# Forgetting attention by pairs of heads: the values stationary in float32, the exponentials moving

## The chip, the cores and the metric

The kernel runs on one core of a Trainium2 chip, alone. The metric is the device time of one execution in microseconds (us); the number to forecast is the median of several executions. The engines are TensorE (PE in the rows; PEld is its weight load), VectorE (DVE), ScalarE (ACT), GpSimd (POOL) and SyncE (SP), which issues the DMAs here. Each engine works through a list of its own, in an order that is fixed when the program is built; the engines meet at semaphores.

## The reference

One layer with two branches on the same projection of x (2048 tokens, 1024 columns), a gate, an output projection, and a last RMSNorm. The change is in the second branch, attention over 8 heads of 64 columns with a forget gate:

```python
h = rmsnorm(x, norm_g[l]);  p = h @ w_in[l]          # 1024 -> 3208 + 1024 gate columns
y_rw  = rwkv7_branch(...)                             # recurrence over time, 8 heads
# fox_branch, per head and block of queries:
q = rmsnorm(heads(p[..., 0:512]), q_g);  k = rmsnorm(heads(p[..., 512:1024]), k_g)
c = jnp.cumsum(jax.nn.log_sigmoid(fl + b_f), axis=1)
s = jnp.einsum('bhqd,bhkd->bhqk', qb, kf) * scale + cb[..., :, None] - c[:, :, None, :]
s = jnp.where(mask, s, -jnp.inf)
o = jnp.einsum('bhqk,bhkd->bhqd', jax.nn.softmax(s, axis=-1), vf)
y = jnp.concatenate([y_rw, y_fox], axis=-1) * jax.nn.silu(gate)
x = x + y @ w_out[l];  return rmsnorm(x, final_g)
```

## The kernel before

The program has three parts. **Part one** projects: the RWKV columns (line 254, `pj_r`) with the work that prepares the recurrence, and between them, as filler, the attention's q, k and v (line 332, `pf`) and the gates (line 254, `pj_g`). **Part two** is the recurrence over 32 chunks of 64 tokens, `chain` (`pX`, `pY`, `pU`, `pS`, lines 737 to 763), which goes step by step from TensorE to VectorE or ScalarE and back; attention is the work that stands between its steps. **Part three** is `out_tile`: 16 tiles of 128 tokens, each with 48 matmuls of 512 columns (line 1111, `po`).

Where an instruction stands on its engine is decided by a scheduler of the framework when the program is built. The source gives the order of priority (`chain_all` ahead of `attend`), the scheduler then mixes the streams by durations it assumes.

Attention has two steps per head. `head_max` finds the largest score of each query: matmuls into `sq` (lines 947 and 950) and a maximum of each on VectorE (line 951). `head_out` then goes through 4 blocks of 512 queries; block `qb_` has `4 * qb_ + 4` tiles `j` of 128 keys. For each tile it forms the scores `st` with two float16 matmuls of 512 columns (lines 998 and 999; the high and low halves of q and k are spread over the rows) and, on the diagonal, a mask (line 1002). ScalarE takes the exponential into float32 `p32` (line 1006), ScalarE or VectorE rounds it to float16 `ph` (lines 1008 and 1010), GpSimd or VectorE forms the rest `pl` (line 1012). TensorE then holds a 128x128 piece of `ph` or `pl` stationary, and the values move through it, 64 or 65 columns in float16:

```python
nc.tensor.matmul(pv[:, qq, 0:65], ph[:, s_], vh[:, j, 0:65], ...)   # line 1016
nc.tensor.matmul(pv[:, qq, 0:64], ph[:, s_], vl[:, j], ...)         # line 1018
nc.tensor.matmul(pv[:, qq, 0:65], pl[:, s_], vh[:, j, 0:65], ...)   # line 1020
```

Column 65 of the values is one, so the sum of the exponentials comes with them. On the diagonal the matrices are narrower: `c0` columns are left out. Heads 0 to 5 go one after the other, heads 6 and 7 block by block together, so that `out_tile` can start.

Of the kernel before, what the change touches and what calls it, by code (L numbers as in the profile page):

```python
# [9 lines left out]
F32 = mybir.dt.float32  # L10
# [25 lines left out]
VS = 2.0 ** -20  # L36
# [3 lines left out]
def hymba_body(tc, x, norm_g, w_in, rw_mu, rw_w_up, rw_w0, rw_a_up, rw_a0, rw_k_k, rw_k_a, rw_r_k,  # L40
# [7 lines left out]
    with ctx:  # L48
# [13 lines left out]
        d_q = [dram(f"d_q{i}", [512, S], F16) for i in range(2)]  # L62
        d_k = [dram(f"d_k{i}", [512, S], F16) for i in range(2)]
        d_v = [dram(f"d_v{i}", [4, 128, 2, 16, 66 - 2 * i], F16) for i in range(2)]
        d_l = dram("d_l", [NB, 128, 2, TB])
        d_yr = dram("d_yr", [512, S])
        d_gate = dram("d_gate", [1024, S])
        d_nc = [dram(f"d_nc{i}", [8, S], F16) for i in range(2)]
        d_gs = dram("d_gs", [4, S], F16)
        d_yf = dram("d_yf", [S, 512])  # L70
# [150 lines left out]
        def load_tiles(name, offs):  # L221

            iall = wp.tile([128, 6], F32, name="ia_" + name, tag="ia", bufs=2)
            ws = [(wp.tile([128, KT, 128], F16, name=f"wh_{name}{i}", tag="wh", bufs=3),
                   wp.tile([128, KT, 128], F16, name=f"wl_{name}{i}", tag="wl", bufs=3)) for i in range(len(offs))]
            prep_w(name, offs, "r", ws, iall)
            return ws, iall
# [58 lines left out]
        def fox_turn(p, b, j0, qkn, qkt):  # L286
# [12 lines left out]
            if j0:  # L299
                pc = slice(p * 128, p * 128 + 128)  # L300
                for i, d in ((0, d_q), (1, d_k)):
                    for a in range(2):
                        nc.sync.dma_start(d[a][pc, b * TB:b * TB + TB], qkt[i][:, a])

        def fox_proj(p, fw, w):
# [10 lines left out]
            for b in range(NB):  # L316
# [3 lines left out]
                vh = F("vh" + u, "vh", (128, 2, 4, 66), F16)  # L320
                vl = F("vl" + u, "vl", (128, 2, 4, 64), F16)
                nc.gpsimd.memset(vh[:, :, :, 64:66], 1.0)
                qkt = [F(f"qkt{u}_{i}", f"qt{i}", (128, 2, TB), F16) for i in range(2)]
                qkn = []
                for j in range(4):
# [20 lines left out]
                    nc.scalar.activation(vh[:, :, j, 0:64], pv, AF.Copy, scale=VS)  # L346
                    nc.vector.scalar_tensor_tensor(vl[:, :, j], pv, VS, vh[:, :, j, 0:64], ALU.mult, ALU.subtract)
# [5 lines left out]
                for i, t in ((0, vh), (1, vl)):  # L353
                    nc.sync.dma_start(d_v[i][p, :, :, 4 * b:4 * b + 4].rearrange("q a j c -> q a (j c)"),
                                      t.rearrange("q a j c -> q a (j c)"))
# [25 lines left out]
        groups = [("f", 0), ("f", 1), ("f", 2), ("g", 0), ("g", 3), ("g", 6), ("f", 3)]  # L381
# [385 lines left out]
        def group_norm(sg, yt):  # L767
# [25 lines left out]
            nc.sync.dma_start(d_yr[:, t0:t0 + 256].rearrange("(p q) t -> q p t", q=128), gt)  # L793
# [36 lines left out]
        with c2:  # L830
# [30 lines left out]
            gs = A("gs", "nct", (32, S // 16), F16)  # L861
            nc.vector.memset(gs, GS)
            nc.sync.dma_start(d_gs[2:4].rearrange("o (j q) -> (o j) q", q=128), gs)
            gs = A("gz", "nct", (32, S // 16), F16)
            nc.vector.memset(gs, 0.0)
            nc.sync.dma_start(d_gs[0:2].rearrange("o (j q) -> (o j) q", q=128), gs)
# [4 lines left out]
            def decay_setup(p):  # L871
# [37 lines left out]
                nch = [A(f"nch{p}_{i}", f"nch{i}", (32, 128), F16) for i in range(2)]  # L909
                nc.vector.tensor_copy(nch[0], nct)  # L910
                nc.vector.tensor_tensor(nch[1], nct, nch[0], ALU.subtract)
                for i in range(2):
                    nc.sync.dma_start(d_nc[i][hs].rearrange("h (j q) -> (h j) q", q=128), nch[i])

            def v_setup(h):

                vi = ap_.tile([128, 1], F32, name=f"vi{h}", tag="vi", bufs=2)
                ts(vi, iscv[:, h:h + 1], 1.0 / VS, ALU.mult)
                vh = ap_.tile([128, 16, 66], F16, name=f"va{h}", tag="va", bufs=2)
                vl = ap_.tile([128, 16, 64], F16, name=f"vb{h}", tag="vb", bufs=2)  # L920
                nc.sync.dma_start(vh, d_v[0][h // 2, :, h % 2])
                nc.sync.dma_start(vl, d_v[1][h // 2, :, h % 2])
                return vh, vl, vi

            def head_max(h):

                qb = ap_.tile([128, S], F16, name=f"qb{h}", tag="qb", bufs=3)
                km = ap_.tile([128, S], F16, name=f"km{h}", tag="km", bufs=2)
                r = slice(h * 64, h * 64 + 64)
                nc.sync.dma_start(qb[0:64], d_q[0][r])  # L930
                nc.sync.dma_start(qb[64:66], d_gs[2:4])
                nc.sync.dma_start(km[0:64], d_k[0][r])
                for i in range(2):
                    nc.sync.dma_start(km[64 + i:65 + i], d_nc[i][h:h + 1])
                mx = ap_.tile([128, 16, 4], F32, name=f"mx{h}", tag="mx", bufs=2)
                nc.vector.memset(mx, -3e38)
                for i in range(16):
                    nb = i // 4 + 1
                    cut = [round((i + 1) * 128 * b / nb / 32) * 32 for b in range(nb + 1)]
                    for b in range(nb):  # L940
# [6 lines left out]
                        nc.tensor.matmul(ps[:, :w], qb[0:66, i * 128:i * 128 + 128], km[0:66, ks],  # L947
# [10 lines left out]
                gh = ap_.tile([16, 128], F16, name=f"gh{h}", tag="gh", bufs=2)  # L958
                gl = ap_.tile([16, 128], F16, name=f"gl{h}", tag="gl", bufs=2)
                nc.vector.tensor_copy(gh, pg)  # L960
                nc.vector.tensor_tensor(gl, pg, gh, ALU.subtract)
                return qb, gh, gl

            def head_loads(h, qb, gh, gl):

                qa = ap_.tile([128, S], F16, name=f"qa{h}", tag="qa", bufs=2)
                ka = ap_.tile([128, S], F16, name=f"ka{h}", tag="ka", bufs=2)
                kb = ap_.tile([128, S], F16, name=f"kb{h}", tag="kb", bufs=2)
                r = slice(h * 64, h * 64 + 64)
                nc.sync.dma_start(qa[0:64], d_q[0][r])  # L970
                nc.sync.dma_start(qa[64:128], d_q[1][r])
                nc.sync.dma_start(ka[0:64], d_k[0][r])
                nc.sync.dma_start(ka[64:128], d_k[0][r])
                nc.sync.dma_start(kb[0:64], d_k[1][r])
                nc.sync.dma_start(kb[64:68], d_gs)
                nc.sync.dma_start(qb[66:67].rearrange("o (j q) -> o j q", q=128), gh)
                nc.sync.dma_start(qb[67:68].rearrange("o (j q) -> o j q", q=128), gl)
                return qa, ka, qb, kb, *v_setup(h)

            def head_out(h, qa, ka, qb, kb, vh, vl, vi, blocks=range(4), last2=False):  # L980
                for qb_ in blocks:
                    nj = 4 * qb_ + 4
                    q0 = qb_ * 512
                    u = f"{h}_{qb_}"
                    be = ap_.tile([128, 16], F32, name="be" + u, tag="be", bufs=2)
                    nc.vector.tensor_scalar(be[:, :nj], c_[:, h, :nj], cref[:, h, 4 * qb_:4 * qb_ + 1], -1.0,
                                            ALU.subtract, ALU.mult)
                    pv = ps_v.tile([128, 4, 66], F32, name="pv" + u, tag="v")
                    for j in range(nj):
                        o = max(j - 4 * qb_, 0)  # L990
# [10 lines left out]
                        if diag:  # L1001
                            nc.tensor.matmul(ps[:, c0:c0 + 128], identb, mkT, start=False, stop=True)
# [155 lines left out]
```

## Time and profile before

| | |
|---|---|
| median of 3 runs | 1707.08 us (1707.0 to 1711.47) |
| the execution that was profiled | 1709.08 us, span 1707.4 us |
| TensorE | busy 1575.2 us, 92% of the span |
| VectorE, ScalarE, GpSimd | 71%, 49%, 45% of the span |
| mean granted clock of TensorE | 0.96 of 2.4 GHz |

The span goes from the first to the last instruction; 1.7 us lie around it. A matmul counts as busy from its start until its result is out, and matmuls overlap, so two that start 0.03 us apart may each be shown as 0.19 us long. How much TensorE can still take is therefore read from the distance between starts, not from its busy share.

### The profile page before, as it was taken

Reading aid. Unit: us, or ns where it says so; the run is one execution under the profiler, and the core shown is the slowest. Engines: PE = TensorE matmul, PEld = TensorE weight load, DVE = VectorE, ACT = ScalarE, POOL = GpSimd, SP = SyncE. Lnnn points to the kernel's source line nnn. Section 1 sums busy time; section 2 is a strip of 40 time slices with the busy share of each in tenths; the row PEclk is TensorE's granted clock in tenths of the full one; section 3 lists DMA queues with packets and bytes.
Section 4 is the critical chain, followed back from the end, with each engine's and each line's share of the span. In section 5 each row is a group of like instructions: output and inputs, shape, how many; then the busy total and the mean of one; then the engine's idle time right before and its main releaser. Section 6 shows DMA issues by size and latency. Waiting matters only on the chain. (4 is left out here: it accounts for less than half of the span.)

```text
span 1707.4 us, 36607 instructions
## 1 busy us (share of the span) xinstructions
PE 1575.2 (92%) x14182; PEld 974.5 (57%) x14182; DVE 1210.0 (71%) x2614; ACT 839.9 (49%) x1583; POOL 766.9 (45%) x838
## 2 busy tenths in 40 slices
PE   4899799899998999999999999899999998899998
PEld 2455355455544564445453566566666665567886
DVE  4866568975888669743844678588999997975443
ACT  5644444445433454445343247566776677564221
POOL 5754554545345543532201135455666666663000
PEclk9899899999998999999999999899999998899999
DMA  6432232233213242322234029666879633733452
GB/s 180 124 100 87 97 114 87 87 112 122 103 69 118 82 143 74 117 96 106 96 102 130 26 63 253 158 150 159 186 169 208 144 99 79 214 99 103 164 173 75
DMA packets 211983, 207.74 MB, mean 122 GB/s; under 512 B 53664, under 2 KB 173472, under 8 KB 211296
## 3 DMA queue, kind: packets, MB, share of 16 engines
q1 hardware_dynamic: 211808, 205.39, 42.1%
q8 instruction: 112, 1.84, 0.5%
q14 instruction: 63, 0.52, 0.1%
HBM read 123.34 MB, written 81.94 MB: 120 GB/s over the span
## 5 line engine op out<-in xcount | busy, mean ns | idle before, releaser
L1012 POOL TENSOR_TENSOR pl<-p,ph 128x512 f16<-128x512 f32 (+3 forms) x216 | 234.5, 1095 | 175.1 <-ACT ph L1010 70.3
L1006 ACT ACTIVATE p<-st,be 128x512 f32<-128x512 f32 (+1 forms) x320 | 193.5, 621 | 125.5 <-PE st L999 32.1
L951 DVE TENSOR_REDUCE mx<-sq 128x1 f32<-128x384 f32 (+6 forms) x320 | 184.5, 600 | 22.3 <-PE sq L947 11.6
L332 PE MATMUL pf<-fh_f,hhi 128*128 128x386 f16 x512 | 171.3, 335 | 2.1 <-DVE fl L348 1.0
L332 PE MATMUL pf<-fl_f,hhi 128*128 128x386 f16 x512 | 170.2, 332 | 1.9 <-POOL fl_f L219 1.9
L332 PE MATMUL pf<-fh_f,hlo 128*128 128x386 f16 x512 | 170.3, 333 | 0.0
L254 PE MATMUL pj_r<-hhi,wh_r 128*128 128x512 f16 x384 | 147.7, 385 | 1.3 <-ACT wh_r L218 1.2
L254 PE MATMUL pj_r<-hlo,wh_r 128*128 128x512 f16 x384 | 147.6, 384 | 0.0
L254 PE MATMUL pj_r<-hhi,wl_r 128*128 128x512 f16 x384 | 147.4, 384 | 0.0
L332 PEld LDWEIGHTS <-hhi 128*128 128x128 f16 x1024 | 100.1, 100 | 78.6 <-issue 14.6
L341 POOL TENSOR_TENSOR fr<-ft,nhalf 128x4 f32<-128x4 f32 x64 | 65.8, 1029 | 173.9 <-DVE ft L101 167.8
L1016 PE MATMUL pv<-va,ph 128*128 128x65 f16 x1088 | 133.4, 197 | 9.6 <-DVE ot L1026 7.6
L1020 PE MATMUL pv<-va,pl 128*128 128x65 f16 x1088 | 130.2, 197 | 4.6 <-POOL pl L1012 2.5
L1018 PE MATMUL pv<-vb,ph 128*128 128x64 f16 x1088 | 132.5, 195 | 0.0
L1010 ACT ACTIVATE ph<-p 128x512 f16<-128x512 f32 (+3 forms) x220 | 121.0, 561 | 13.1 <-PE pv L1020 6.8
L254 PEld LDWEIGHTS <-wh_r 128*128 128x128 f16 x768 | 74.9, 99 | 87.3 <-issue 6.5
L999 PE MATMUL st<-qb,kb 68*128 68x512 f16 (+1 forms) x320 | 114.6, 361 | 10.4 <-DMA qb<-gl 10.2
L998 PE MATMUL st<-qa,ka 128*128 128x512 f16 (+1 forms) x320 | 114.3, 360 | 6.9 <-ACT p L1006 3.9
L1016 PEld LDWEIGHTS <-ph 128*128 128x128 f16 x1088 | 102.9, 99 | 26.6 <-DVE ot L1026 9.9
L947 PE MATMUL sq<-km,qb 66*128 66x384 f16 (+6 forms) x320 | 107.0, 353 | 10.1 <-DVE mx L951 5.2
L1020 PEld LDWEIGHTS <-pl 128*128 128x128 f16 x1088 | 102.6, 99 | 22.6 <-POOL pl L1012 5.7
L1018 PEld LDWEIGHTS <-ph 128*128 128x128 f16 x1088 | 103.0, 100 | 7.7 <-issue 1.2
(378 smaller groups left out, 4068.4 us busy)
## 6 DMA issues: line engine op xcount, KB each, us to landing
d_ga<-ga SPq DMA_DIRECT2D x32, 256.0 KB
d_gl<-gl SPq DMA_DIRECT2D x32, 256.0 KB
d_nk<-nkt SPq DMA_DIRECT2D x32, 256.0 KB
d_gate<-gv SPq DMA_DIRECT2D x32, 256.0 KB
G<-d_ga SPq DMA_DIRECT2D x32, 256.0 KB
G<-d_gl SPq DMA_DIRECT2D x32, 256.0 KB
NK<-d_nk SPq DMA_DIRECT2D x16, 512.0 KB
xr<-in_x_dram SPq DMA_DIRECT2D x16, 512.0 KB
```

Source lines behind the costliest of these rows:

```text
L254: nc.tensor.matmul(ps, a[:, kt, o:o + 128], h[:, kt, :], start=n == 0, stop=n == 3 * KT - 1)
L332: nc.tensor.matmul(ps, a[:, kt, js], w[:, kt, :], start=n == 0, stop=n == 3 * KT - 1)
L947: nc.tensor.matmul(ps[:, :w], qb[0:66, i * 128:i * 128 + 128], km[0:66, ks], start=True, stop=not last)
L951: nc.vector.tensor_reduce(mx[:, i, b:b + 1], ps[:, :w], AX.X, ALU.max)
L998: nc.tensor.matmul(ps[:, c0:], ka[:, k0:k0 + 128], qa[:, q0 + c0:q0 + 512], start=True, stop=False)
L999: nc.tensor.matmul(ps[:, c0:], kb[0:68, k0:k0 + 128], qb[0:68, q0 + c0:q0 + 512], start=False, stop=not diag)
L1006: nc.scalar.activation(p32[:, c0:], ps[:, c0:], AF.Exp, bias=be[:, j:j + 1])
L1010: nc.scalar.activation(ph[:, c0:], p32[:, c0:], AF.Copy)
L1012: eng.tensor_tensor(pl[:, c0:], p32[:, c0:], ph[:, c0:], ALU.subtract)
L1016: nc.tensor.matmul(pv[:, qq, 0:65], ph[:, s_], vh[:, j, 0:65], start=j == 0 and qq == 0, stop=False, skip_group_check=True)
L1018: nc.tensor.matmul(pv[:, qq, 0:64], ph[:, s_], vl[:, j], start=False, stop=False, skip_group_check=True)
L1020: nc.tensor.matmul(pv[:, qq, 0:65], pl[:, s_], vh[:, j, 0:65], start=False, stop=fin, skip_group_check=True)
```

## The change

Attention goes by pairs of heads. `p32` is not split any more. The values of a tile of keys, 128x64 in float32, are now the stationary operand, head 0 of the pair in the left half of the array's columns and head 1 in the right half, and the float32 exponentials move through them, up to 512 columns in one matmul. The result has 64 columns of head 0 in partitions 0 to 63 and those of head 1 in 64 to 127, which is the layout that the output projection needs. The sums of the exponentials are formed by adding the tiles on VectorE and GpSimd into `acc` (the first tile's), and a float32 matmul with ones brings the sum over keys (`normalise`). Its reciprocal is `exp(-ln)` with one step of refinement; the gate is multiplied in here, so that `out_tile` loads one finished `y`.

```diff
-                        nc.scalar.activation(p32[:, c0:], ps[:, c0:], AF.Exp, bias=be[:, j:j + 1])
-                        if j % 4 < 2 if last2 else j % 4 == 2:
-                            nc.vector.tensor_copy(ph[:, c0:], p32[:, c0:])
-                        else:
-                            nc.scalar.activation(ph[:, c0:], p32[:, c0:], AF.Copy)
-                        eng = nc.vector if j % 3 == 1 else nc.gpsimd
-                        eng.tensor_tensor(pl[:, c0:], p32[:, c0:], ph[:, c0:], ALU.subtract)
-                        for qq in range(o, 4):
...
-                            nc.tensor.matmul(pv[:, qq, 0:65], ph[:, s_], vh[:, j, 0:65],
-                                             start=j == 0 and qq == 0, stop=False, skip_group_check=True)
...
+                    def values(j, c0, pt):
+                        for h, (o0, o1) in enumerate(HR):
+                            nc.tensor.matmul(pv[o0:o1, c0:], ops[h][2][:, j, :], pt[h][:, c0:],
+                                             start=j == 0, stop=j == nj - 1, skip_group_check=True)
+                        if j:
+                            for h in range(2):
+                                e = nc.vector if (h if alt else (2 * j + h) % 3 == 0) else nc.gpsimd
+                                e.tensor_tensor(acc[h][:, c0:], acc[h][:, c0:], pt[h][:, c0:], ALU.add)
...
+                            nc.scalar.activation(pt[h][:, c0:], ps[:, c0:], AF.Exp, bias=be[h][:, j:j + 1])
...
+                        pend.append((j, c0, pt))
+                        if j:
+                            values(*pend.pop(0))
+                        if j == 2 and rest:
+                            rest.pop()()
+                    values(*pend.pop(0))
+                    yv = ap_.tile([128, 512], F32, name=f"yv{u}", tag="yv", bufs=2)
+                    nc.scalar.activation(yv, pv, AF.Copy, scale=vi)
+                    nc.gpsimd.tensor_tensor(yv, yv, gt, ALU.mult)
...
+            def normalise(u, yv, acc, rows, qs):
+
+                pd = ps_s.tile([128, 512], F32, name=f"pd{u}", tag="s")
+                for h, (o0, o1) in enumerate(HR):
+                    nc.tensor.matmul(pd[o0:o1], ones[:, 0:64], acc[h], start=True, stop=True)
+                rd = ap_.tile([128, 512], F32, name=f"rd{u}", tag="rd")
+                nc.scalar.activation(rd, pd, AF.Ln)
+                nc.scalar.activation(rd, rd, AF.Exp, scale=-1.0)
+                nc.gpsimd.tensor_tensor(yv, yv, rd, ALU.mult)
+                nc.vector.tensor_tensor(rd, pd, rd, ALU.mult)
+                nc.vector.scalar_tensor_tensor(yv, rd, 2.0, yv, ALU.subtract, ALU.mult)
+                nc.sync.dma_start(d_y[rows, qs], yv)
```

Beside this, q and k are stored per head with their extra rows, so that each is loaded with fewer, larger DMAs (q per block of queries, 4 buffers each); in part one the values are stored once in float32 instead of twice in float16 (one VectorE instruction less per tile of line 332); `out_tile` loses four transposes, one multiplication and two loads per tile; the gates of the attention's columns are projected earlier; the weight tiles `wh` and `wl` come from another pool.

The order of TensorE's instructions before, in part two, in attention of head 3 (names: `st3_1_3` scores of head 3, block 1, tile 3; `pv3_0` its result of block 0; `sq4` the maxima of head 4):

```order
L998 LDWEIGHTS ka3_14779
L998 MATMUL st3_1_3_15932<-qa3_14778,ka3_14779 128x512
L999 LDWEIGHTS kb3_14780
L999 MATMUL st3_1_3_15932<-qb3_10130,kb3_14780 128x512
L947 LDWEIGHTS qb4_14623
L947 MATMUL sq4_9_1_14689<-km4_14624,qb4_14623 128x448
L1016 LDWEIGHTS ph3_0_0_15795
L1016 MATMUL pv3_0_15789<-va3_14791,ph3_0_0_15795 128x65
L1018 LDWEIGHTS ph3_0_0_15795
L1018 MATMUL pv3_0_15789<-vb3_14792,ph3_0_0_15795 128x64
L1020 LDWEIGHTS pl3_0_0_15796
L1020 MATMUL pv3_0_15789<-va3_14791,pl3_0_0_15796 128x65
```

All of it uses the whole width of the array, and three short matmuls with the values follow one another for each 128 queries.

The same place after the change, attention of pair 1 (`va2` and `va3` are the values of its two heads, `pv1_2` the result of block 2 for both, in 64 partitions each; `pd1_1` the sums of block 1; `pU18` is a step of the recurrence):

```order
L1022 MATMUL st1_2_2_1_14200<-qb1_2_1_14167,kb3_13717 128x512
L1004 MATMUL pv1_2_14171<-p321_2_1_1_14183,va3_13719 64x512
L744 MATMUL pU18_12630<-xs18_12619,zc4_12323 64x64 x8
L964 MATMUL pd1_1_14208<-p321_1_0_0_13833,ones_8320 64x512
L964 MATMUL pd1_1_14208<-p321_1_0_1_13834,ones_8320 64x512
L1004 MATMUL pv1_2_14171<-p321_2_2_0_14194,va2_13713 64x512
L1021 LDWEIGHTS ka2_13709
L1021 MATMUL st1_2_3_0_14220<-qa1_2_0_14157,ka2_13709 128x512
L1022 LDWEIGHTS kb2_13711
L1022 MATMUL st1_2_3_0_14220<-qb1_2_0_14160,kb2_13711 128x512
L1004 MATMUL pv1_2_14171<-p321_2_2_1_14195,va3_13719 64x512
L932 LDWEIGHTS qm5_8_14048
```

The matmul of tile 2 with `va2` and the one with `va3`, which the source writes one after the other, stand apart here, with scores of the whole width between them.

After the recurrence, in pair 3, some of them stand together:

```order
L1004 MATMUL pv3_2_15923<-p323_2_0_0_15924,va6_15653 64x512
L1004 MATMUL pv3_2_15923<-p323_2_0_1_15925,va7_15659 64x512
L1004 MATMUL pv3_2_15923<-p323_2_1_0_15934,va6_15653 64x512
L1004 MATMUL pv3_2_15923<-p323_2_1_1_15935,va7_15659 64x512
L1021 LDWEIGHTS ka7_15655
```

Here the left and the right half follow each other directly. Over the whole program there are 320 matmuls with values and 32 with ones; 58 pairs of a left and a right one stand together, and 236 stand alone.

## Rows read from the trace of the kernel before

**Rows 1.** The page's first part: busy us, share, instructions of each engine.

```profile
PE 1575.2 (92%) x14182; PEld 974.5 (57%) x14182; DVE 1210.0 (71%) x2614; ACT 839.9 (49%) x1583; POOL 766.9 (45%) x838
```

**Rows 2.** Stretches: busy us (count) of PE, PEld, DVE, ACT, POOL; clock; DMA share; GB/s.

```profile
0.00:1019.00 1019.00, 937.61 (x6389) 515.02 (x6390) 688.43 (x1587) 448.40 (x824) 431.03 (x512) 0.96 0.31 101
1019.00:1707.00 688.00, 637.54 (x7795) 459.47 (x7793) 521.57 (x1028) 391.55 (x760) 335.84 (x327) 0.96 0.60 152
```

**Rows 3.** Busy time by stretch: a piece of part two, one of part three.

```profile
1250.00:1300.00 50.00, 48.11 (x799) 34.24 (x800) 49.27 (x101) 32.52 (x64) 30.43 (x31) 1.00 0.78 176
1650.00:1700.00 50.00, 50.00 (x228) 41.05 (x226) 20.02 (x36) 10.61 (x25) 2.69 (x4) 1.00 0.32 111
```

**Rows 4.** Waits of TensorE from 1019 us on, the two longest.

```profile
PE st L999 <- DMA qb<-gl: 10.2, 2, 7.5
PE pv L1016 <- DVE ot L1026: 7.6, 5, 2.2
```

**Rows 5.** Groups by line from 1019 us on, TensorE: count, busy us, mean ns.

```profile
L1016 PE MATMUL pv<-va,ph 128*128 128x65 f16 x1078 | 132.0, 197 | 9.6 <-DVE ot L1026 7.6 <-DVE ph L1008 1.5 <-ACT ph L1010 0.4
...
L998 PE MATMUL st<-qa,ka 128*128 128x512 f16 (+3 forms) x312 | 111.7, 360 | 6.1 <-ACT p L1006 3.9 <-issue 1.8
L1111 PE MATMUL po<-woh,yh 128*128 128x512 f32 x256 | 102.0, 400 | 0.8 <-DVE woh L1078 0.4 <-ACT yh L1101 0.4
...
L947 PE MATMUL sq<-km,qb 66*128 66x448 f16 (+5 forms) x271 | 90.5, 355 | 5.3 <-DVE mx L951 3.6 <-DMA d_yr<-gg 0.8 <-DMA km<-d_nc 0.4
...
L737 PE MATMUL pX<-SV,G 128*64 128x64 f32 x512 | 25.0, 233 | 0.0
...
L1095 PE MATMUL pt<-ident,yf 128*128 128x128 f32 x64 | 9.9, 272 | 0.0
```

**Rows 6.** Timeline of TensorE: start us, us, what.

```profile
1198.76 0.38 PE L998 MATMUL st<-qa,ka 128*128 128x512 f16 x1
1198.98 0.38 PE L999 MATMUL st<-qb,kb 68*128 68x512 f16 x1
1199.29 0.69 PE L737 MATMUL pX<-SV,G 128*64 128x64 f32 x16
```

**Rows 7.** The same timeline, asked from the end of that group on.

```profile
1199.74 0.23 PE L737 MATMUL pX<-SV,G 128*64 128x64 f32 x2
1199.91 0.20 PE L1020 MATMUL pv<-va,pl 128*128 128x65 f16 x1
```

**Rows 8.** Timeline of TensorE, twelve starts between the two rows left out.

```profile
1201.12 0.20 PE L1016 MATMUL pv<-va,ph 128*128 128x65 f16 x1
...
1201.52 0.19 PE L1018 MATMUL pv<-vb,ph 128*128 128x64 f16 x1
```

**Rows 9.** Timeline of TensorE in part one, float32 in four quarters of the array.

```profile
353.51 0.28 PE L541 MATMUL pb<-ga,bk 64*64 64x128 f32 x2
353.53 0.28 PE L544 MATMUL pk<-ga,bk 64*64 64x128 f32 x2
353.62 0.28 PE L541 MATMUL pb<-ga,bk 64*64 64x128 f32 x2
353.64 0.28 PE L544 MATMUL pk<-ga,bk 64*64 64x128 f32 x2
```

**Rows 10.** Groups by line from 1019 us on, the other engines.

```profile
L1012 POOL TENSOR_TENSOR pl<-p,ph 128x512 f16<-128x512 f32 (+3 forms) x212 | 231.1, 1100 | 171.3 <-ACT ph L1010 69.4 <-DVE ph L1008 42.1 <-PE pv L1020 21.7
...
L1010 ACT ACTIVATE ph<-p 128x512 f16<-128x512 f32 (+2 forms) x215 | 118.3, 562 | 13.1 <-PE pv L1020 6.8 <-PE pv L1018 3.4
...
L1012 DVE TENSOR_TENSOR pl<-p,ph 128x512 f16<-128x512 f32 (+3 forms) x102 | 86.1, 844 | 8.5 <-ACT ph L1010 4.6 <-POOL pl L1012 1.9 <-PE st L999 0.7
L1008 DVE CAST ph<-p 128x512 f16<-128x512 f32 (+1 forms) x98 | 55.8, 575 | 20.1 <-ACT p L1006 12.5 <-PE pv L1020 4.0 <-PE pv L1018 3.1
...
L792 POOL TENSOR_TENSOR gg<-ysq,gg 128x512 f32<-128x512 f32 x16 | 22.7, 1420 | 14.1 <-DVE ysq L790 12.5 <-DVE gm L955 0.8 <-PE pv L1020 0.8
L787 DVE TENSOR_TENSOR ysq<-yt,ysq 128x512 f32<-128x512 f32 x16 | 13.5, 843 | 0.2 <-ACT ysq L786 0.2
```

More of the change, by code (lines that the diff above doesn't have):

```diff
@@ new lines, in hymba_body @@
+            rest = []
+            def normalise(u, yv, acc, rows, qs):
[9 more added lines that the diff above has]
+                nc.sync.dma_start(d_y[rows, qs], yv)
@@ L981, in head_out, with pair_out @@
+            def pair_out(p, ops, alt, blocks):
+                vi = ap_.tile([128, 1], F32, name=f"vi{p}", tag="vi", bufs=2)
+                for h, (o0, o1) in enumerate(HR):
+                    ts(vi[o0:o1], iscv[o0:o1, 2 * p + h:2 * p + h + 1], -1.0, ALU.mult, eng=nc.gpsimd)
                 for qb_ in blocks:
@@ new lines, in pair_out @@
+                    u = f"{p}_{qb_}"
+                    be, q1s, q2s = [], [], []
+                    for h in range(2):
+                        hd_ = 2 * p + h
+                        b = ap_.tile([128, 16], F32, name=f"be{u}_{h}", tag="be", bufs=4)
+                        nc.vector.tensor_scalar(b[:, :nj], c_[:, hd_, :nj], cref[:, hd_, 4 * qb_:4 * qb_ + 1], -1.0,
+                                                ALU.subtract, ALU.mult)
+                        be.append(b)
+                        q1 = ap_.tile([128, 512], F16, name=f"qa{u}_{h}", tag="qa", bufs=4)
+                        for o0, o1 in HR:
+                            nc.sync.dma_start(q1[o0:o1], d_qh[hd_, 0:64, qs])
+                        q2 = ap_.tile([128, 512], F16, name=f"qb{u}_{h}", tag="qb", bufs=4)
+                        nc.sync.dma_start(q2[0:66], d_ql[hd_, :, qs])
+                        q1s.append(q1)
+                        q2s.append(q2)
@@ new lines, in pair_out @@
+                        for h in range(2):
+                            kk, km = ops[h][0:2]
+                            psp, tg = (ps_q, "q") if alt and h else (ps_s, "s")
+                            ps = psp.tile([128, 512], F32, name=f"st{u}_{j}_{h}", tag=tg)
+                            nc.tensor.matmul(ps[:, c0:], kk[:, k0:k0 + 128], q1s[h][:, c0:], start=True, stop=False)
+                            nc.tensor.matmul(ps[:, c0:], km[0:66, k0:k0 + 128], q2s[h][0:66, c0:],
+                                             start=False, stop=not diag)
+                            if diag:
+                                nc.tensor.matmul(ps[:, c0:c0 + 128], identb, mkT, start=False, stop=True)
+                            nc.scalar.activation(pt[h][:, c0:], ps[:, c0:], AF.Exp, bias=be[h][:, j:j + 1])
@@ new lines, in pair_out, with top, bottom @@
+                    rest.append(partial(normalise, u, yv, acc, slice(512 + p * 128, 640 + p * 128), qs))
+            def heads():
+                def top(h):
+                    if h < 8:
+                        if h % 2 or h == 0:
+                            if (h + 1) // 2 < 4:
+                                decay_setup((h + 1) // 2)
+                        head_max(h)
+                def bottom(p, blocks):
+                    if blocks[0] == 0:
+                        for h in (2 * p, 2 * p + 1):
+                            ops[h] = head_loads(h)
+                    h = 2 * p
+                    pair_out(p, ops[h:h + 2], p == 3, blocks)
+                ops = [None] * 8
+                top(0)
+                yield
+                top(1)
+                yield
+                for p in range(4):
+                    top(2 * p + 2)
+                    bottom(p, (0, 1))
+                    top(2 * p + 3)
+                    bottom(p, (2, 3))
+                    if p == 3:
+                        rest.pop()()
```

199 lines of the change are left out of this document (66 added, 133 removed).

## The prediction

> **What bounds the kernel now.** The page's first part comes first: TensorE is busy for 1575 us, 92% of the span, the others for at most 71% [rows 1]. That figure counts matmuls until their results are out, so I split the span where the last projection ends, at 1019 us, and ask how much TensorE could still take behind it, where the change acts. There lie 688 us, of which TensorE is busy for 637.5 [rows 2].
>
> Distances between starts tell what it really does there. A float16 matmul of 512 columns takes 0.22 us, by two scores [rows 6] and by 228 matmuls in 50 us of part three, where TensorE never pauses [rows 3]; that is 0.43 ns a column. The short matmuls with the values follow each other every 0.031 us, 13 steps in 0.40 us [rows 8]; their weight loads are hidden. The recurrence runs in part of the array: the first 14 of 16 records start within 0.45 us, two by two, so a pair takes 0.064 us [rows 6, 7]. Entering such a group costs 0.09 us more than the next score would (0.31 against 0.22) [rows 6]; from its last two records to the next whole-width matmul 0.17 us pass, 0.10 more than a pair takes [rows 7]. I count 0.095 us for each change of width.
>
> With the order's counts the 688 us hold: scores and masks 124 us (294,912 columns in all, 312 of 320 tiles here [rows 5]); maxima 57 (155,648 columns, 271 of 320 [rows 5]); values 3,234 x 0.031 = 100; recurrence 1,272 x 0.064 = 82; output 768 x 0.22 = 169; the rest (sums of squares, transposes) 16; changes of width 374 x 0.095 = 36. Together 584 us. So 104 us are free on TensorE, spread out: its longest named waits are 10.2 and 7.6 us [rows 4]. In part two VectorE is at least as tight, 49.3 us of 50 busy [rows 3], so there neither engine alone sets the pace; in part three it is TensorE.
>
> **The change part by part.** *Taken from TensorE:* the 3,234 short matmuls, 100 us, and the 64 transposes of the output tiles, at most their 9.9 us in flight [rows 5]; I take 7.
>
> *Given to TensorE:* 320 float32 matmuls with values and 32 with ones, 155,648 columns. The trace has no such matmul with 512 columns. The recurrence's `pX` has the same form, 128 rows and 64 columns of the array in float32, and shows 512 records for 256 matmuls [rows 5]: two records each. In part one, four records of 128 columns in four quarters of the array start almost together, and the next four 0.11 us later [rows 9]. By that a record of 512 columns takes 0.44 us and a matmul 0.88. By the 64-column pairs it would be 8 x 0.064 x 2 = 1.02; by the step from 64 to 128 columns (0.046 us), 2 x (0.064 + 7 x 0.046) = 0.77. I take 0.86, close to rows 9, whose records are the longer ones.
>
> The two heads use the two halves of the columns and overlap if they stand next to each other, as the records of `pX` do, which start in pairs [rows 6, 7]. The order says that mostly they don't: 58 pairs stand together (25,728 columns each half), 236 matmuls alone (105,216 columns), with whole-width scores behind them, and the next whole-width matmul waits until the half is through [rows 7]. So 130,944 columns / 512 x 0.86 = 220 us, between 197 and 263 by the two bounds. Were all 352 in pairs, it would be 77,824 / 512 x 0.86 = 131 us.
>
> The Trainium skill has a rule for the gain: "TensorEngine Tiling (Array Packing)", Performance Considerations, gives column tiling with a stationary side of at most 64 columns a factor of two, which is the 131 us. It has another that speaks against it here: "TensorE: Matmul & The Clock Gate", Part 3, says that matmuls start and end in program order, so a half that stands alone finds no partner, which is the 220 us.
>
> *Changes of width:* 732 instead of 374 from the projection's end on, 358 x 0.095 = 34 us. *Order:* a few tiles of scores and maxima that stood ahead of the projection's end now stand behind it: 4 us more here and as much less before. TensorE behind the projection: 584 - 100 - 7 + 220 + 34 + 4 = 735 us. That is more than the 688 us that this stretch took with all its waits.
>
> *The other engines* get room. ScalarE loses the roundings, 118 us, and gets 48 instructions in the shape of one of them, about 30 us: 392 becomes some 304 [rows 2, 10]. VectorE loses 86 and 56 us of splitting and gets 108 of the 288 additions at 0.84 us or less and 32 steps of the normalisation: 522 becomes about 500 at most, less by the division of `ot` that I leave out [rows 2, 10]. GpSimd loses 231 us and gets 180 additions and 32 products at 1.42 us or less: 336 becomes at most 406 [rows 2, 10]. All stay far below 735, so their gains are worth nothing where TensorE is full; they only make its waits fewer. The additions into `acc` are off the path: the values' matmul reads the exponentials, not the sums, and the sum is asked for a block later. The DMAs carry about the same bytes; with 0.60 of the DMA engines' time taken in the stretch [rows 2] I cost them at nothing, covered by the longer stretch; if a pair's first q comes late, it is again a wait like the 10.2 us over two times [rows 4].
>
> *Waits that remain:* none at best, 104 us at worst. TensorE's list is now fuller and the others emptier, so I take 30. *The part before the projection's end:* 1019 less the 4 us, 1015; one VectorE instruction less per tile frees an engine busy 688 of 1019 us [rows 2] and is costed at nothing.
>
> Sum: 1015 + 735 + 30 = 1780 us of span, against 1707.4. The profiled execution is 1.7 us above its span and 2.0 above the median of the runs; both fall out, so **1780 us**, 4% slower.
>
> **The rivals.** *A, the halves overlap anyway (faster).* The array or its queue lets a half that stands alone run beside other work, for instance the left one beside the next right one past the scores between. Then values and sums cost 131 instead of 220 us, and the stretch 646 + 30: 1015 + 676 = 1691. For it: the pairs of `pX` overlap fully. Against it: after a group in part of the array the next whole-width matmul starts 0.10 us late, not early [rows 7]. It decides where 73 of the 89 us come back, four fifths of the lone columns. The skill's factor of two, named above, is this case. Chance 0.11.
>
> *B, the free time takes it all (no change).* Waits vanish and a matmul costs 0.77: 735 - 23 + 1015 = 1727; even this is slower than before, so a time within 0.3% needs half of A as well. Chance 0.04.
>
> *C, the waits stay (still slower).* TensorE now has matmuls of 0.86 us in its list, and behind each one the recurrence's next step queues. If recurrence and exponentials then wait for one another as often as now, the 104 us remain: 1015 + 735 + 104 = 1854. For it: 227 of the 352 float32 matmuls stand between the first and the last step of the recurrence, whose results VectorE and ScalarE wait for. Against it: these two have become emptier, and the tile's exponentials are asked for only one tile later. Chance 0.13.
>
> *The forecast*, 1735 to 1825: chance 0.72.
>
> **How the numbers follow.** A measurement of this kernel tells about 0.3% from no change, some 5 us. Slower: forecast and C, 0.85; same: 0.04 with B; faster: A, 0.11. The range runs from 1727 (price and waits at their lower ends) to 1855 (C): A, half of B and a little above C lie outside. The price's upper bound alone would give 1823.
>
> **What the profile would show.** The matmuls with the values as records of 0.43 us between starts, two per matmul, 0.86 us for a lone half and the same for a pair together; 0.095 us at each change of width; a TensorE that never pauses from 1015 us on, with VectorE, ScalarE and GpSimd emptier; part three beginning later. If lone halves take 0.43 us, A is right; if TensorE pauses for 100 us, C is. The forecast would also be wrong if float32 streams faster at 512 columns than at 128, which no row shows.

## The result, and the profile after

| | median of runs (lowest to highest) | profiled execution | its span |
|---|---|---|---|
| before | 1709.28 us (1707.0 to 1712.1) | 1709.08 us | 1707.4 us |
| after | 1876.72 us (1876.07 to 1878.18) | 1876.21 us | 1874.2 us |

The ratio is 1.098 (95% interval 1.0957 to 1.1003): slower, as forecast, but by 167 us and not by 71; 1877 lies above the range (1727 to 1855).

The page of the kernel after, its first and fourth part, which answers to [rows 1]:

```profile
span 1874.2 us, 30633 instructions
...
PE 1732.3 (92%) x11558; PEld 913.3 (49%) x11558; DVE 1148.1 (61%) x2350; ACT 764.7 (41%) x1395; POOL 781.8 (42%) x834
...
PE 43%; DMA 4%; DVE 1%; SPq 1%; issue 0%; ACT 0%; DVEq 0%; POOLq 0%; ACTq 0%
```

TensorE has the same share as before and everyone else less. The stretches before and behind the projection's end, now at 1022 us, answer to [rows 2] (columns as there):

```profile
0.00:1022.00 1022.00, 933.22 (x6333) 513.34 (x6334) 677.03 (x1518) 442.37 (x813) 428.04 (x495) 0.97 0.32 102
1022.00:1874.00 852.00, 799.10 (x5228) 399.93 (x5225) 471.05 (x833) 322.32 (x583) 353.81 (x339) 0.95 0.47 124
```

Nearly all of the loss lies behind the projection, 852 us in place of 688; the projection itself ends 3 us later. The same stretch in two pieces:

```profile
1022.00:1125.00 103.00, 69.71 (x590) 39.05 (x587) 46.91 (x109) 17.48 (x36) 17.90 (x23) 0.64 0.81 171
1125.00:1850.00 725.00, 712.26 (x4566) 347.02 (x4565) 417.81 (x712) 301.95 (x539) 334.81 (x315) 1.00 0.44 120
```

For the first 103 us TensorE stands still for a third of the time, at a granted clock of 0.64 on average; then it is busy for 712 of 725 us at a granted clock of 1.00, the full 2.4 GHz. Its waits from 1022 us on, which answer to [rows 4] (total, times, longest):

```profile
PE st L1022 <- DMA qb<-d_ql: 21.5, 2, 20.7
PE pX L732 <- DMA d_ql<-qkt: 5.9, 1, 5.9
PE sq L932 <- DMA qm<-d_qh: 5.3, 4, 2.8
PE pU L744 <- DMA zc<-d_z: 4.1, 1, 4.1
```

The longest is pair 0's first score, held up from 1084 to 1105 us by the query operand with head 1's maxima. The values' matmuls in the timeline (start, us in flight, what):

```profile
1155.39 0.38 PE L1022 MATMUL st<-qb,kb 66*128 66x512 f16 x1
1155.69 1.07 PE L1004 MATMUL pv<-p,va 128*64 128x512 f32 x2
1156.70 0.39 PE L1021 MATMUL st<-qa,ka 128*128 128x512 f16 x1
...
1159.40 0.33 PE L758 MATMUL pY<-AR,SV 64*64 64x64 f32 x2
1159.66 0.36 PE L932 MATMUL sq<-km,qm 68*128 68x448 f16 x1
```

A lone value matmul is two records, and from its start to the next whole-width matmul 1.01 us pass; it also starts 0.30 us behind the score where a score would start after 0.22 [rows 6].

For a balance that doesn't count overlap twice I went through TensorE's records behind the projection's end in order of start, and gave each the distance to the next start, less what lay behind its own end ("nothing in flight"). Sums in us; e1, e2 and so on are the runs of the next section. The last two columns are the mean granted clock of the stretch and an estimate of what its time at the granted clock of 0.50 cost: for each record there, its distance less the mean distance of records of the same form at 1.00 in the same run. That cost is contained in the columns of work.

| kernel | scores, maxima | values, sums | recurrence | output | rest | nothing in flight | clock | cost of half clock |
|---|---|---|---|---|---|---|---|---|
| before | 203 | 113 | 119 | 181 | 21 | 44 | 0.96 | 18 |
| after | 227 | 249 | 127 | 181 | 13 | 48 | 0.95 | 23 |
| e1 | 224 | 167 | 125 | 181 | 15 | 54 | 0.93 | 36 |
| e2 | 254 | 110 | 117 | 181 | 19 | 27 | 0.98 | 11 |
| e13 | 307 | 106 | 114 | 181 | 19 | 18 | 0.99 | 5 |
| e8 | 287 | 251 | 130 | 181 | 13 | 41 | 0.95 | 25 |
| e6 | 236 | 256 | 135 | 180 | 15 | 45 | 0.93 | 41 |
| e14 | 229 | 251 | 128 | 181 | 15 | 39 | 0.95 | 27 |
| e9 | 226 | 163 | 123 | 181 | 16 | 59 | 0.92 | 43 |
| e10 | 217 | 157 | 116 | 180 | 15 | 51 | 0.95 | 26 |
| e12 | 243 | 62 | 125 | 183 | 20 | 81 | 0.87 | 65 |
| e15 | 200 | 102 | 118 | 183 | 23 | 64 | 0.92 | 36 |

Work rose by 797 - 637 = 160 us, where the prediction's terms make 735 - 584 = 151. Nothing in flight stayed: 44 became 48. So did the cost of the half clock, 18 and 23: it stood in the kernel before as well, and the prediction's prices, all from rows at the full clock, leave it out.

### The profile page after: what moved, and what is told of

It reads as the page before. It is cut to its first block, busy times and chain, and to the rows that moved or that the text cites. A ratio compares the mean times of both kernels' runs of the same rounds, so it can differ in the third digit from the quotient of the medians.

```text
span 1874.2 us, 30633 instructions
## 1 busy us (share of the span) xinstructions
PE 1732.3 (92%) x11558; PEld 913.3 (49%) x11558; DVE 1148.1 (61%) x2350; ACT 764.7 (41%) x1395; POOL 781.8 (42%) x834
## 5 line engine op out<-in xcount | busy, mean ns | idle before, releaser
L1026 ACT ACTIVATE p<-st,be 128x512 f32<-128x512 f32 (+3 forms) x320 | 193.9, 622 | 262.3 <-PE st L1022 141.9
L1009 POOL TENSOR_TENSOR p<-p,p 128x512 f32<-128x512 f32 (+3 forms) x180 | 208.0, 1159 | 206.3 <-ACT p L1026 179.5
L1004 PE MATMUL pv<-p,va 128*64 128x512 f32 (+3 forms) x640 | 270.1, 556 | 0.2
L936 DVE TENSOR_REDUCE mx<-sq 128x1 f32<-128x512 f32 (+6 forms) x320 | 186.1, 605 | 102.1 <-PE sq L932 58.4
L1022 PE MATMUL st<-qb,kb 66*128 66x512 f16 (+3 forms) x320 | 112.1, 352 | 21.5 <-DMA qb<-d_ql 21.5
L1021 PE MATMUL st<-qa,ka 128*128 128x512 f16 (+3 forms) x320 | 113.6, 357 | 8.9 <-DMA qa<-d_qh 3.9
L932 PE MATMUL sq<-km,qm 68*128 68x512 f16 (+6 forms) x320 | 108.3, 374 | 13.1 <-DMA qm<-d_qh 5.3
L1123 PE MATMUL po<-woh,yh 128*128 128x512 f32 x256 | 101.7, 397 | 0.0
L1123 PE MATMUL po<-wol,yh 128*128 128x512 f32 x256 | 101.4, 396 | 0.0
L1123 PE MATMUL po<-woh,yl 128*128 128x512 f32 x256 | 100.4, 393 | 0.0
```

The source lines that it names most:

```text
L932: nc.tensor.matmul(ps[:, :w], qm[0:68, i % 8 * 128:i % 8 * 128 + 128], km[0:68, ks], start=True, stop=not last)
L936: nc.vector.tensor_reduce(mx[:, i, b:b + 1], ps[:, :w], AX.X, ALU.max)
L1004: nc.tensor.matmul(pv[o0:o1, c0:], ops[h][2][:, j, :], pt[h][:, c0:], start=j == 0, stop=j == nj - 1, skip_group_check=True)
L1009: e.tensor_tensor(acc[h][:, c0:], acc[h][:, c0:], pt[h][:, c0:], ALU.add)
L1021: nc.tensor.matmul(ps[:, c0:], kk[:, k0:k0 + 128], q1s[h][:, c0:], start=True, stop=False)
L1022: nc.tensor.matmul(ps[:, c0:], km[0:66, k0:k0 + 128], q2s[h][0:66, c0:], start=False, stop=not diag)
```

## The experiments

Thirteen kernels ran, each beside the kernel before. Where runs were not timed beside each other, differences of a few us are read by their ratios to the kernel before.

### e1_dep: value matmuls next to each other

```
+ with tc.high_priority():
      for h, (o0, o1) in enumerate(HR):
-         nc.tensor.matmul(pv[o0:o1, c0:], ...)
+         mm = nc.tensor.matmul(pv[o0:o1, c0:], ...)
+         if h == 0:   # ex: the second head's exponential
+             tc.add_manual_dep(mm.ins, ex, ...)
```

> The first of a tile's two value matmuls waits for the second head's exponential too, and both go ahead of other work, so that they stand next to each other in TensorE's stream: 170 adjacent pairs and 12 lone ones (the sums' matmuls counted) in place of 58 and 236, 728 changes of tile width in place of 912. Theory 1 (TensorE sets the pace from 1125 us on, a lone value matmul takes as long as an adjacent pair, some 1.0 us at 512 columns by the spacing in the trace, about 0.9 at the mean 446 columns of the lone ones, and a change of width 0.095): 112 fewer slots x 0.9 and 184 x 0.095 less, -117 us, so 1760 us (1745 to 1775). Theory 2 (the halves don't work at the same time even when adjacent): only the changes of width, some -17 us, 1860. Theory 3 (TensorE is late for other engines or transfers, which keep their pace): half or less of the 117, 1820 to 1870.

Measured: 1795.69 us, ratio 1.050 (1.0462 to 1.0538). That is 81 us less than the changed kernel: most of theory 1's 117, though above its range (1745 to 1775), too much for theory 2, and below theory 3's range. The timeline of this run:

```profile
1162.52 1.08 PE L1005 MATMUL pv<-p,va 128*64 128x512 f32 x4
1163.54 0.39 PE L1024 MATMUL st<-qa,ka 128*128 128x512 f16 x1
```

Four records, two matmuls, take 1.02 us to the next start, where the changed kernel's lone two records took 1.01. Values and sums fall from 249 to 167 us in the balance. Of the 36 us that are missing from the 117, some 13 are the half clock (36 in place of 23 in the balance) and 6 more time with nothing in flight. A wait of this run is new: the pair waits for the second exponential (groups by line: busy us, mean ns, idle before).

```profile
L1005 PE MATMUL pv<-p,va 128*64 128x512 f32 (+3 forms) x640 | 162.3, 569 | 13.1 <-ACT p L1029 12.7
```

### e2_double and e13_triple: what the kernel before can take up

```
- nc.tensor.matmul(ps[:, c0:], ka[...], qa[...], start=True, stop=False)
+ for i in range(2):        # range(3) and stop=i < 2 in e13_triple
+     nc.tensor.matmul(ps[:, c0:], ka[...], qa[...], start=True, stop=i == 0)
```

> The kernel before with the first score matmul of each tile issued twice (the first result is overwritten, the output is unchanged): 320 more whole-width matmuls, 139,264 columns, at the 0.22 us for 512 columns of the trace 60 us, and up to 10 us more for their weight loads. Theory 1 (the kernel before has next to no free time on TensorE behind the projection: 44 us with nothing in flight, and those in waits that stay): +55 to +70 us, 1765 to 1780. The prediction's own step (104 us free, of which the change takes some 70 and leaves 30 in waits): the 60 to 70 us go into free time for the most part, +0 to +25 us, 1710 to 1735.

> The kernel before with the first score matmul of each tile issued three times; issued twice it took 1736 us for 1711, so that of some 55 us of work added 25 to 30 showed. Theory 1 (the kernel before can take up some 30 us on TensorE, and that is used up by the first copy): the second copy costs 45 to 60 us more, 1780 to 1796. Theory 2 (it takes up half of what is added up to 74 us or more, as the prediction's sum has it): 25 to 30 us more, 1760 to 1768.

Measured: 1735.87 us (ratio 1.0143, 1.0116 to 1.0171) and 1780.18 us (1.041, 1.0372 to 1.0447). The first copy cost 25 us, at the upper edge of the prediction's step and far from theory 1; the second cost 44, at the lower edge of its theory 1. Each copy adds some 52 us of scores in the balance, and nothing in flight goes from 44 to 27 to 18. The stretch behind the projection in e2, where TensorE is busy for 681 of 716 us:

```profile
1024.00:1740.00 716.00, 681.28 (x8107) 483.54 (x8105) 509.00 (x1027) 396.74 (x758) 332.21 (x326) 0.98 0.57 146
```

The same in e13, 727 of 752:

```profile
1024.00:1776.00 752.00, 727.22 (x8413) 506.75 (x8411) 511.82 (x1025) 400.79 (x758) 325.74 (x326) 0.99 0.54 139
```

So the kernel before can take up some 35 us of score matmuls (104 added, 69 shown), most of it with the first copy: not none, and not 74. By the balance, 26 us come out of the time with nothing in flight; the other records become 14 us shorter, since less of the stretch runs at half clock (cost 18, then 5); and the projection's end, 4 us later, takes 4 back.

### e8_double: what the changed kernel can take up

The same edit on the changed kernel's `kk`, `q1s` matmul.

> The changed kernel with the first score matmul of each tile issued twice, the same extra work that cost the kernel before 25 us (1736 against 1711). Theory 1 (in the changed kernel TensorE works without a break from 1125 us on, so that nothing more can be taken up there): +50 to +65 us, 1927 to 1942. Theory 2 (it takes up as much as the kernel before did): +20 to +30 us, 1897 to 1907.

Measured: 1933.58 us, ratio 1.1286 (1.1253 to 1.1318): 52 us more than the changed kernel by the ratios, 57 by the medians, for 60 added in the balance. Theory 1 holds: next to nothing is taken up. Two stretches of this run:

```profile
1021.00:1125.00 104.00, 75.45 (x629) 42.25 (x628) 49.38 (x113) 17.98 (x37) 20.25 (x25) 0.64 0.84 173
1125.00:1905.00 780.00, 769.96 (x4833) 374.88 (x4830) 410.84 (x705) 305.04 (x538) 330.75 (x313) 0.99 0.41 110
```

The standstill at the start is there as before: TensorE's next instruction in its order, a score, waits 18.8 us there for the query operand, and the copies stand behind it.

### e4_noadd: without the sums

The additions `acc + p32` are left out (one addition of 1 for each row of blocks in their place), so the sums are not the reference's.

> The changed kernel with the tile-by-tile sums of exponentials left out (each head's accumulator only gets 1 added once per row of blocks), so that VectorE and GpSimd lose some 290 additions of up to 512 elements, and the exponentials' buffers come free with the value matmul; the matmuls are all there. Theory 1 (the sums run beside TensorE, which sets the pace): 0 to -10 us, 1867 to 1877. Theory 2 (the sums set the pace: they hold the exponentials' buffers and VectorE and GpSimd): -30 us or more, 1847 or less.

Measured: 1868.24 us, ratio 1.0927 (1.0897 to 1.0957); 8 us less. Theory 1: the sums hide behind TensorE.

### e3_queue: the late operand from another queue

```
- nc.sync.dma_start(d_ql[h, 64:66]..., gh)
+ (nc.scalar if h < 2 else nc.sync).dma_start(d_ql[h, 64:66]..., gh)
- nc.sync.dma_start(q2[0:66], d_ql[hd_, :, qs])
+ (nc.sync if p else nc.scalar).dma_start(q2[0:66], d_ql[hd_, :, qs])
```

> The changed kernel with the store of heads 0 and 1's maxima and the loads of pair 0's second query operands issued from ScalarE's queue instead of SyncE's. In the trace after, head 1's maxima are ready at 1081 us, their store is issued at 1094 behind recurrence loads, the operands are issued at 1102.6 and TensorE waits for them 20.7 us, to 1104.5. Theory 1 (the place in SyncE's queue makes it late): -12 to -18 us, 1859 to 1865. Theory 2 (the DMA engines, 77 to 113% busy there, make it late wherever it is issued): -5 us at most, 1872 to 1877.

Measured: 1882.16 us, ratio 1.100 (1.0975 to 1.1026), no gain, and above the ranges of both theories. The maxima are ready at 1082 us in this run; ScalarE's timeline goes on:

```profile
1093.77 0.33 ACTq L946 DMA_DIRECT2D d_ql<-gh  x1
1094.15 0.63 ACT L88 ACTIVATE ysh<-ysq 128x512 fp32r<-128x512 f32 x1 [12.12 <-DMA G<-d_ga]
1101.86 2.52 ACTq L994 DMA_DIRECT2D qb<-d_ql  x3
```

On the new queue the store is issued hardly earlier than on SyncE's in the changed kernel (1094.3), and the load at 1101.9 (1102.6). In the 78 us ahead the DMA engines were busy nearly all the time:

```profile
1027.00:1105.00 78.00, 49.45 (x448) 30.01 (x447) 37.07 (x88) 7.61 (x18) 9.38 (x13) 0.59 0.98 205
```

But the place in a queue wasn't all that held the store. In the trace the DMAs of both queues use eight semaphores in turn, and ScalarE's wait of 12.12 us ends with a load of the recurrence (`G<-d_ga`): SyncE had issued it at 1084.1 with the store's semaphore, its last part landed at 1093.70, and 0.07 us later the store was issued. In the changed kernel the store stood right behind a load (`SV<-d_vn`) whose issue took SyncE until 1094.25. So the run doesn't show that the DMA engines make the operand late wherever it is issued; it exchanged one obstacle for another. A store free of both was not tested.

### e6_quarter, e7_depquarter, e14_odd: maxima in time for the first block

The maxima of one head are made available after every fourth query tile (`max_out` holds the lines from `gm` to the store of `gh`, for query tiles i0 to i1):

```
+ step_ = 4 if h == 1 else 16      # h % 2 in e14_odd and e10_odd
  for i in range(16):
      ...
+     if (i + 1) % step_ == 0:
+         max_out(h, mx, i + 1 - step_, i + 1)
```

> The changed kernel with head 1's maxima reduced, stored and made available by quarters of the queries, so that pair 0's first row of blocks needs a quarter of them and its score matmuls follow soon after the projection's end instead of at 1104 us. Everything else as in the changed kernel. Theory 1 (behind the projection the changed kernel has nothing but the recurrence, bound by its loads, and head 1's maxima for 84 us: TensorE is busy 51 of them, at a granted clock of 0.5 to 0.64, with one wait of 20.7 us): -20 to -45 us, 1832 to 1857. Theory 2 (the DMA engines set the pace of that stretch whatever else is there, the time only moves): 0 to -10 us, 1867 to 1877.

> Adjacent pairs of value matmuls (as in the run that had 1796 us) and head 1's maxima by quarters together. Theory 1 (both losses are real and separate): 1796 less 20 to 45 us, 1750 to 1776. Theory 2 (the start was only covered up): 1786 to 1796. Faster than the kernel before (1711) in neither: 170 pairs of two passes stay, some 150 us of TensorE against the 113 us of the kernel before's value matmuls.

> The changed kernel with the maxima by quarters of the queries for the second head of every pair, the value matmuls left as they are, one by one for the most part. With head 1's quarters alone the changed kernel took 1895 us for 1877; with adjacent value matmuls two tiles at a time, quarters for every pair gave 24 us against quarters for head 1 alone. Theory 1 (the loss at the changes of pair is there whatever the value matmuls cost): 20 to 40 us below the changed kernel, 1837 to 1857. Theory 2 (with lone value matmuls TensorE is so far behind that the maxima are done in time anyway, but at the start): 0 to -10 us, 1867 to 1877.

Measured: e6 1894.59 us (ratio 1.1044, 1.1003 to 1.1085), e7 1806.04 (1.0533, 1.0503 to 1.0563), e14 1870.49 (1.0939, 1.0914 to 1.0963). The first two are misses for both theories, the third is theory 2's. In e6 the start is mended, and a stretch of the same kind stands 200 us later:

```profile
1022.00:1125.00 103.00, 93.71 (x654) 39.96 (x651) 52.47 (x124) 34.85 (x64) 37.05 (x41) 0.87 0.76 175
...
1225.00:1325.00 100.00, 77.40 (x676) 43.43 (x676) 53.49 (x108) 22.52 (x43) 23.69 (x28) 0.63 0.68 148
```

In that stretch a matmul of maxima waits 10.9 us for its operand, and a score 7.2 us for its query operand (waits from the projection's end on; total, times, longest):

```profile
PE sq L946 <- DMA qm<-d_qh: 16.8, 3, 10.9
PE st L1028 <- DMA qb<-d_ql: 7.2, 1, 7.2
```

So the 20.7 us were not a loss of their own that an earlier operand gives back. By the balance nothing in flight is 3 us less than in the changed kernel; what makes e6 slower is the half clock, which costs some 41 us in place of 23. From 1303 to 1311 us the granted clock is 0.50, and a lone value matmul takes 1.90 us to the next start there, against 1.01 in the changed kernel's rows:

```profile
1308.83 1.97 PE L1010 MATMUL pv<-p,va 128*64 128x512 f32 x2
1310.73 0.39 PE L1027 MATMUL st<-qa,ka 128*128 128x256 f16 x1
```

### e9_two and e10_odd: two tiles at a time, quarters for every pair

```
- if j: values(*pend.pop(0))
+ if j % 2: values(pend, ex.ins.name); pend = []   # four matmuls in a row
```

> As the run with adjacent pairs and quarters, but the value matmuls of two tiles are issued together, four in a row, each waiting for the last exponential of the two tiles: 648 changes of tile width in place of 736. Theory 1 (a change of width costs 0.095 us): -8 us against that run. Theory 2 (two tiles' exponentials hold four of the six buffers until then, and ScalarE waits for them): +10 us or more against it.

> Adjacent value matmuls, two tiles at a time, and the maxima by quarters of the queries for the second head of every pair, not only of the first: a pair's first row of blocks then needs a quarter of those maxima. The runs with quarters for head 1 alone took the wait at the start away and got a stretch of the same kind 200 us later, where pair 1 waits for head 3's maxima (TensorE at 77 of 100 us, granted clock 0.63). Theory 1 (a pair that needs two heads' maxima before its first score leaves TensorE with little at each change of pair; the quarters mend it everywhere): -20 to -45 us against the run with two tiles at a time (1794), 1750 to 1775. Theory 2 (the maxima have to be worked off somewhere, and only the place moves): 1785 to 1800.

Measured: e9 1794.1 us (1.0468, 1.0442 to 1.0495), 12 less than e7, more than the 8 that 88 changes of width at 0.095 make; e10 1770.48 (1.034, 1.031 to 1.0371), 24 less than e9, within theory 1's range and near its lower edge. Here quarters pay, where in e14 they hardly did: by the balance some 17 of the 24 us are time at half clock that e9 has and e10 hasn't (43, then 26), and 7 are time with nothing in flight. e14 has 27 where the changed kernel has 23, so there it had nothing of the kind to win. e10 is the best of these with float32 values, still 59 us slower than before.

### e12_f16: one pass instead of two

Values and exponentials are single float16 (`F16` tiles, values scaled by 2^-20), so their low parts are left out.

> As the run with quarters for every pair, but values and exponentials are single float16 numbers in place of float32 (their low parts are left out, so the output is coarser), so that a value matmul is one pass of the array instead of two records; 4 copies in place of the first tile's sum come to it. Theory 1 (the two passes of float32 are what is left of the loss: adjacent value matmuls take some 143 us, 70 of them for the second pass): -60 to -75 us against that run. Theory 2 (with adjacent pairs TensorE isn't the bound any more; maxima, recurrence or transfers are): -30 us or less.

Measured: 1742.09 us, ratio 1.0176 (1.0142 to 1.021), 28 less than e10, in theory 2's range. Values and sums fall by 95 us in the balance, but scores and maxima rise by 26, the recurrence by 9, and nothing in flight by 30. The rise of the scores and the recurrence is the half clock: the granted clock of the stretch fell from 0.95 to 0.87, which costs 65 us in place of 26. At the full clock the work would have fallen by some 90 us (an estimate: 687 less 26, against 634 less 65). The longest waits:

```profile
PE sq L947 <- DMA qm<-d_qh: 17.4, 6, 6.3
PE sq L947 <- DVE mx L951: 11.5, 16, 2.7
PE pg L920 <- DVE gm L918: 8.0, 7, 3.1
```

Even with 62 us for values and sums, against 113 before, e12 is 1.4 to 2.1% slower than the kernel before.

### e15_before: quarters in the kernel before

The same `max_out`, for every head, with its results stored into `qb` directly.

> The kernel before with every head's maxima reduced and put into its query operand by quarters of the queries, so that a head's first row of blocks needs a quarter of them. Theory 1 (the wait of 7.5 us for the operand at the start and some of the shorter waits at changes of head go, and the next waits don't take their place): -6 to -12 us, 1699 to 1705 for 1711. Theory 2 (the free time is taken up by other waits, or the additional small operations on VectorE and transfers cost as much): -3 to +5 us.

Measured: 1751.1 us, ratio 1.0241 (1.0218 to 1.0264): 39 us slower, a miss for both. The projection now ends 35 us later (at 1054 us), because earlier scores go ahead of it. Behind it the work is only 11 us less (626 for 637). At the full clock it would be some 29 less, by the balance; the half clock costs 36 us in place of 18, and nothing in flight is 20 us more:

```profile
1019.00:1054.00 35.00, 35.00 (x364) 23.00 (x363) 29.76 (x82) 21.25 (x46) 17.28 (x18) 1.00 0.30 74
1054.00:1751.00 697.00, 626.27 (x7329) 445.37 (x7327) 500.98 (x1076) 356.16 (x696) 308.11 (x302) 0.92 0.57 147
```

The longest wait is one that the additional steps brought (transposes of the maxima that wait for VectorE):

```profile
PE pg L932 <- DVE gm L930: 12.0, 8, 5.0
```

## Why the prediction was wrong

**Price and number of the value matmuls: right.** Values and sums were put at 220 us, and the way out of their groups at 0.095 each. The balance has 249 for both: they stand in 302 groups, of which 220 end at a whole-width matmul (the others at a step of the recurrence), and these ways out make 220 x 0.095 = 21, which leaves 228. A lone half takes as long as a pair: shown by the two timelines (1.01 and 1.02 us) and by e1's 81 us. Rival A is out: the right half starts beside the left one only when it is the next instruction. The Trainium skill's two rules, weighed in the prediction, agree with this: the factor two of "TensorEngine Tiling (Array Packing)", Performance Considerations, for the pairs (1.02 us for two), and the program order of "TensorE: Matmul & The Clock Gate", Part 3, for the lone ones (1.01 us for one).

**"So 104 us are free on TensorE": this step failed.** The 688 us less 584 of work were read as free time. By the balance, 637 us of it were work, 44 nothing in flight, and 7 lay behind the last matmul. The 53 us that the sum missed came from prices taken in the tightest places, at the full clock, and used everywhere. The recurrence has 19 more (82 and the ways out, against 119): a group of two records takes 0.26 us to the next matmul, as the last two rows of the timeline of after show, where a pair and a change of width made 0.16. Output has 12 more (181 against 169), the values 13, scores with their entries and the rest 9. Some 18 of these 53 us are the half clock, by the estimate in the balance: 8 of the scores' and the rest's, 5 of the values', 4 of the recurrence's, 1 of the output's. The mean granted clock of 0.96 stood in the rows [rows 2], and the sum put it at nothing without a reason. What makes up the other 35 us is shown only in part. The same was missing from the 735 for after: its work is 797, with 23 us of half clock in it.

**"Waits that remain: I take 30": wrong as well.** This let 74 us of the added work go into free time. The kernel before can take up some 35 us of scores (e2, e13). The changed kernel took up next to nothing: 48 us without a matmul in flight remain, 33 of them in the first 103 us, and work added to it shows almost in full (e8). That is nearest to rival C's outcome, the waits stay, which had 0.13, but not by its mechanism: from 1125 us on, where nearly all of the lone value matmuls stand, only some 14 us are without a matmul in flight. That its 1854 comes within 1.2% of the measured time is luck: it has 104 us of waits where 48 + 7 stand, and lacks the 62 of work. Sum of the errors: 62 of work (797 against 735), 25 of waits and of the end behind the last matmul (48 + 7 against 30), 7 for the projection's end (1022 against 1015), and 2 between the span and the execution's time: 96 us in all with rounding, from 1780 to 1876.

**What fills the first 103 us.** A pair needs both heads' maxima before its first score of the second head, and after the projection's end head 1's are still to be done, with the DMA engines taken by the recurrence's loads (a share of 0.81 in these 103 us); the prediction had this as "if a pair's first q comes late, it is again a wait like the 10.2 us". It is 20.7 us and comes in a stretch at a granted clock of 0.64. But e6 and e14 show that mending it moves it, and the sum of nothing in flight stays between 39 and 48 us in every variant with lone values. That the quarters gave 24 us in e10 and 6 in e14 goes with the half clock, which they shortened in the one and not in the other; why they did so is not settled.

**The other engines** were off the path as said: e4 shows 8 us for all sums. In e12 the half clock takes back 39 of the some 90 us that float16 saves, and nothing in flight 30; its waits are for the operands and the reductions of the maxima. What would remove them is not settled. No version beat the kernel before.

## What to carry to other kernels

Before calling the rest of a stretch free, add up the engine's distances from start to start over the whole stretch; a sum of best prices times counts makes free time out of what it leaves out. A mean granted clock below 1.00 is such a term: part of the work costs nearly twice its price there. Then ask which of the waits the new work can fill: only work that is ready then. A matmul in half of the array cost as much here as two side by side (1.01 and 1.02 us), so a split by halves is worth what the order of instructions keeps adjacent; read that from the order, and make one half wait for the other's input if the scheduler doesn't keep them together.

## What the hardware showed unexpectedly

TensorE ran at half its clock (granted 0.50, 1.2 GHz) in a stretch in which it was busy throughout, behind one in which it was busy for 15.5 of 28 us (the kernel after):

```profile
1022.00:1050.00 28.00, 15.47 (x95) 7.26 (x93) 15.01 (x42) 3.38 (x8) 3.20 (x4) 0.64 0.84 178
1050.00:1075.00 25.00, 25.00 (x246) 16.19 (x246) 14.77 (x28) 1.91 (x5) 3.69 (x6) 0.50 1.13 220
```

A float16 matmul of the same 64 by 512 form takes one record in place of float32's two, and much less than half the time. Four in a row take 0.55 us to the next matmul in e12 and 1.87 in e10, at a granted clock of 1.00 in both. First e12, then e10, where each matmul is two records:

```profile
1327.09 0.62 PE L1014 MATMUL pv<-p,va 128*64 128x512 f16 x4
1327.64 0.39 PE L1035 MATMUL st<-qa,ka 128*128 128x512 f16 x1
```

```profile
1271.10 1.94 PE L1012 MATMUL pv<-p,va 128*64 128x512 f32 x8
1272.97 0.39 PE L1030 MATMUL st<-qa,ka 128*128 128x512 f16 x1
```

The expectation for e12 had put half of the values' time, 70 us, on the second record; the values' own matmuls fell from 139 to 43 us.
